# A Hymba decoder step: leaving the 16 meta tokens out of the stages that only feed y

## The chip, the cores and the metric

The kernel runs on one core of a Trainium2 chip. The metric is the device time of one execution in microseconds (us); lower is better. The engines are TensorE (PE; its weight loads are listed as PEld), VectorE (DVE), ScalarE (ACT), GpSimd (POOL) and SyncE (SP), which issues nearly all DMAs.

## The reference

One decoder layer with shared weights for a prompt of 1024 tokens, in front of which 16 learned meta tokens are put, and for 8 sample tokens with their own states. Together 1048 tokens of width 1024, float32:

```
h += 0.5 * SwiGLU_1(rmsnorm(h))              # 1024 -> 2816 -> 1024
u  = rmsnorm(h) @ w_in                       # q, f, i, g (4 heads of 128), z, x/B/C, dt
HGRN2, 4 heads: S_t = diag(f_t) S_{t-1} + k_t v_t^T, o_t = S_t^T q_t
                out = rmsnorm(o) * w * silu(g)
Mamba-2, 8 heads of 64: conv(4) + silu on x/B/C, scan over the tokens, y_t = h_t C_t + D x_t
                out = rmsnorm(y * silu(z)) * w
h += concat(hgrn, mamba) @ w_out
h += 0.5 * SwiGLU_2(rmsnorm(h))
y = rmsnorm(h)                               # the 16 meta tokens are dropped from y_prompt
```

Outputs are y for the prompt and the samples, and the states after the last token. The meta tokens reach the outputs only through the two recurrences and the convolution: through f, k = 1 − f, i, x, B, C and dt of their positions. Their q, g and z, their rows of the output projection, of the second FFN and of the last norm reach no output.

## The kernel before

All activations stand with the 128 features of a block on the partitions and tokens along the free axis, in the order meta, prompt, samples: T = 1048 columns. Tiles of the pool `big` are 1056 columns wide, 30 with the tag `u` and 8 with the tag `s`.

**Products.** A float32 product is made of three matmuls in float32r (`mm3`, lines 141 to 146): high part of the weights by high part of the tokens (line 144), high by low (145), low by high (146). The weights are split on ScalarE (cast, 138) and VectorE (subtraction, 139), so are the tokens. Each matmul loads 128x128 weights and streams the token columns of one chunk.

**The two FFNs** (`ffn`, line 743) use one level of Strassen's scheme in Winograd's form: seven products where a plain split would have eight. The tokens are cut into four quarters of Q = T/4 = 262 columns; quarters (0, 1) and (2, 3) make two lanes, and the scheme joins the quarters of a lane. `pair` (462) makes gate and up of 128 hidden features: 7 products, each of 4 blocks of 128 for either lane, 262 columns at a time. There are 22 pairs. The products are put together on VectorE by `post` (485), multiplied by the norm's factors (`times_r`, 480), and the hidden values are stored to DRAM by `Hidden` (558). `down` (620) reads them back for each of the 7 products of the down projection (`DORDER`), splits them (607, 611) and adds the results to the tiles of h (697). The order of the FFN's instructions on PE, DVE, ACT and SP is written out by hand as steps (`Steps`, 352): `S.before(i, fn)` puts work ahead of step i. `first2` (1854) and `after3` (1904) place the start and the end of the second FFN. After the last product `Final` (1584) and `LastFinal` (1617) transpose h by tiles of 128 tokens, make the last norm and store y; `token_rows` (867) says which rows of a tile go to which output. Tiles 4, 5 and 6 come last.

**The mixer** stands between the FFNs and is ordered by a scheduler, which interleaves projections and scans. `proj` (335) makes one unit of 128 output features in three chunks of columns, (0, 350), (350, 350), (700, 348), with 8 x 3 matmuls each. `ssm_project` (1002) makes x, B and C (8 units) and dt, `ssm_scan` (1142) the Mamba scan in nine chunks of tokens, `ssm_gate` (1288) the four units of z and their gate on y, `ssm_norm` (1306) the grouped norm. For each of the four heads `hgrn_project` (1328) makes q, f and i, `hgrn_scan` (1384) the recurrence over 1040 tokens, a second call of `hgrn_project` the gate g, and `hgrn_out` (1541) norm and gate. The projections that wait their turn fill TensorE between the steps of the scans. The parts of the eight samples are jobs on GpSimd (for HGRN lines 1528 to 1530, read by the matmuls of line 1533) that are slipped in. Two of the four gated heads and two of the tiles of y are spilled to DRAM (`spill`, 1789) and read back split (`split_spilled`, 1792). `out_proj` (1561) multiplies by w_out a quarter at a time and adds to h (1574), which was spilled after the first FFN and is loaded again (1825); `Norm` (187) makes the factors of the second FFN's norm.

Of the kernel before, what the change touches and what calls it, by code (L numbers as in the profile page):

```python
# [29 lines left out]
CHUNKS = [(0, 350), (350, 350), (700, 348)]  # L30
CW = 350
# [33 lines left out]
class Core:  # L65
    def __init__(self, ctx, tc):
# [10 lines left out]
        self.n = 0  # L77
        self.banks_ = ent(ExitStack())
        self.banks(1)

# [90 lines left out]
def rstd_wide(K, v, r, after):  # L171
# [4 lines left out]
    with K.tc.issue_after(ld.ins):  # L176
        parts = [(v[:, s : s + T // 2], r[:, s : s + T // 2]) for s in (0, T // 2)]
# [9 lines left out]
class Norm:  # L187
# [8 lines left out]
    def r(self, q):  # L196
        if self.spread:
            return self.spread.quarter(q)
        return self.rt[q // 2][:, (q % 2) * Q : (q % 2) * Q + Q]

    def add(self, k, q):
        K = self.K
        hs = self.h[k][:, q * Q : q * Q + Q]
        if q not in self.sq:
            self.sq[q] = K.t(Q)
            self.an = K.nc.scalar.activation(self.sq[q], hs, AF.Square)
        else:
            t = K.t(Q)
# [3 lines left out]
    def begin(self, q, table=True):  # L212
        K = self.K
        if not self.spread and q // 2 not in self.rt:
            self.rt[q // 2] = K.t(2 * Q)
        ps = K.psm()
        K.nc.tensor.matmul(ps[:, :Q], K.ones[D], self.sq[q], start=True, stop=True)
        self.newton[q] = K.rstd(self.r(q), ps[:, :Q], Q, self.an if table else None)
# [8 lines left out]
    def begin_half(self, half):  # L227
# [3 lines left out]
        ps = [K.psm()[:, :Q] for i in range(2)]  # L231
        r, l = K.t(2 * Q), K.t(2 * Q)
        for i in range(2):
            nc.tensor.matmul(ps[i], K.ones[D], self.sq[2 * half + i], start=True, stop=True)
            nc.scalar.activation(l[:, i * Q : i * Q + Q], ps[i], AF.Ln, bias=K.eps)
        nc.scalar.activation(r, l, AF.Exp, scale=-0.5, bias=K.lna)

        def newton():
            nc.vector.scalar_tensor_tensor(l, r, -1.0, r, ALU.mult, ALU.mult)
            for i in range(2):  # L240
                li = l[:, i * Q : i * Q + Q]
                nc.vector.scalar_tensor_tensor(li, ps[i], EPS, li, ALU.add, ALU.mult)
            out = self.spread.tile()[:, half * 2 * Q : half * 2 * Q + 2 * Q]
# [5 lines left out]
class Spread:  # L249
# [6 lines left out]
    def tile(self):  # L256
        if self.t is None:
            self.t = self.K.slot("u", T)
        return self.t

    def quarter(self, q):
        return self.tile()[:, q * Q : q * Q + Q]
# [10 lines left out]
def plain_x(K, norm, wcol, q):  # L273

    cs = slice(q * Q, q * Q + Q)
    xn = {}

    def job(k):
        if k < KT:
            xn[k] = K.t(Q)  # L280
# [16 lines left out]
class Blocks:  # L297
# [6 lines left out]
    def new(self, p):  # L304
        self.b[p] = self.K.slot("u", T)
        return self.b[p]

    def scaled(self, h, wcol, ps):

        for p in ps:  # L310
# [3 lines left out]
            for k in range(4):  # L314
                self.K.nc.scalar.activation(t[:, k * Q : k * Q + Q], h[k0 + k][:, q * Q : q * Q + Q], AF.Identity, scale=wcol[:, k0 + k : k0 + k + 1])
# [7 lines left out]
    def cast(self, p):  # L323
        hi = self.K.slot("u", T, F32R)
# [3 lines left out]
    def low(self, p):  # L328
        hi = self.op[p][0]
        lo = self.K.slot("u", T, F32R)  # L330
# [4 lines left out]
def proj(K, wh, wl, evac, chunks=(0, 1, 2)):  # L335

    for c in chunks:
        c0, w = CHUNKS[c]
# [6 lines left out]
def proj_first(K, units):  # L345

    for c in range(3):
# [78 lines left out]
class Unit:  # L426
# [6 lines left out]
    def bank(self, p, cs, mis):  # L433

        b = {2: 1, 3: 5, 4: 7}.get(p, p)
        if (b, cs) not in self.ps:
            K = self.K
            if len(cs) == 2:
                self.ps[b, cs] = K.psum2()[:, :, :Q]
            else:  # L440
                self.ps[b, cs] = (K.psm() if mis and b == 7 else K.psum())[:, None, :Q]
# [20 lines left out]
def pair(K, S, wg, wu, f, ops, spread, hid, late_r, first=None):  # L462
# [12 lines left out]
    def temp(n, cs):  # L475
        if n not in tm:
            tm[n] = halves(K.t(2 * Q))
# [41 lines left out]
    def product_(n, cs):  # L519
        if "h" not in tm:  # L520
            tm["h"] = True
            hid.append(K.slot("s", T))
        nc.vector.tensor_mul(halves(hid[0][:, n * 2 * Q : n * 2 * Q + 2 * Q])[:, cs], temp(f"g{n}", cs), temp(f"u{n}", cs))
# [34 lines left out]
class Hidden:  # L558


    def __init__(self, K):
        self.K = K
        self.d = {p: K.dram.tile([P, 2, FP, Q], F32, name=K.uid("hd")) for p in ORDER}

    def jobs(self, S, i, hid, e0, e1):
# [4 lines left out]
        def block(n):  # L570

            return hid[n // 2][0][:, n % 2 * 2 * Q : n % 2 * 2 * Q + 2 * Q]
# [4 lines left out]
        def sub(p, x, y):  # L577
            s = {5: 0, 6: 0, 7: 1, 4: 1}[p]
            if s not in t:
                t[s] = K.slot("s", T)  # L580
            o = (p in (6, 4)) * 2 * Q
            b[p] = t[s][:, o : o + 2 * Q]
# [12 lines left out]
    def load(self, S, p, at):  # L595
# [4 lines left out]
        def load(g, c):  # L600
            i, n = GROUPS[g]
            op[c][g] = K.slot("u", n * Q, F32R), K.slot("u", n * Q, F32R)
# [17 lines left out]
def down(K, S, wdv, hidden, src, h, after):  # L620
# [6 lines left out]
    def tiles(j):  # L627
        for _ in range(2):
            h.append(K.slot("s", T))
            hs.append(h[-1].rearrange("p (c n t) -> p c n t", c=2, n=2))  # L630

    def residual(o, at):
        box = []

        def load():
            box.append(K.slot("u", T))
# [66 lines left out]
    for a, p in enumerate(DORDER):  # L703
# [6 lines left out]
        if a < 6:  # L710
            for j in range(KT // 2):
                box = []
                for g in range(3):
                    pieces(p, j, g, b + 6 * j + 2 * g, None)
                    for c in range(2):

                        def mm(p=p, j=j, g=g, c=c, op=op, box=box):
                            if not box:
                                box.append(K.psum2()[:, :, :Q])
# [3 lines left out]
        else:  # L723
# [6 lines left out]
            for c in range(2):  # L730
                for j in range(KT // 2):
                    box = []
                    for g in range(3):

                        def mm(p=p, j=j, g=g, c=c, op=op, box=box):
                            if not box:
                                box.append(K.psum()[:, :Q])
# [1223 lines left out]
```

## Time and profile before

| | us |
|---|---|
| median of 3 runs (2028.59 to 2029.81) | 2029.59 |
| the profiled execution | 2029.82 |
| its span, first to last instruction | 2028.1 |

The page of the profile gives the busy time of each engine, the chain of work that ended last, and the costliest groups of instructions with line, tiles and shapes (partitions x elements). The views of the trace that are used below: busy time of the engines in stretches of the span, given in us from its start, with the number of instructions in brackets; groups of instructions by form; waits of an engine by what ended them (total, times, longest); the instructions of one engine in order of time. TensorE's granted clock is a share of full speed. Records of matmuls overlap each other: the next starts before the last has ended.

### The profile page before, as it was taken

The page shows a single profiled execution, that of the slowest core. Times are in us where ns is not written, and L with a number is a line of the kernel's source. Part 1 is how long each engine was busy: PE and PEld are TensorE (multiplying, and loading weights), DVE is VectorE, ACT ScalarE, POOL GpSimd, SP SyncE. Part 2 cuts the span into 40 slices and gives each one's busy share as a digit, 9 for nine tenths or more (in the row PEclk, how much of TensorE's full clock was granted, in tenths as well). Part 3 has the DMA queues.
Part 4 walks back from the last instruction along what each step waited for, and adds up shares of the span by engine and source line. Part 5 has one row for each costly group of instructions (what it writes and reads, how often), then busy time and mean ns, then how long its engine had stood idle before and what let it go on. Part 6 is the DMA issues. An engine that isn't in the chain of part 4 may idle for free.

```text
span 2028.1 us, 40739 instructions
## 1 busy us (share of the span) xinstructions
PE 1958.5 (97%) x16647; PEld 1912.4 (94%) x16647; DVE 1468.5 (72%) x2437; ACT 822.3 (41%) x1528; POOL 153.2 (8%) x197
## 2 busy tenths in 40 slices
PE   6999999999999999979999999999999999999997
PEld 6999999999999999968989889999999999999997
DVE  7777777777688686598454556887777777768973
ACT  6522222224534553564534444752222222354352
POOL 3000000000002210231010111200000000000000
PEclk8999999999999999999999999999999999999999
DMA  6233342325976621263120335224232333587851
GB/s 213 74 98 98 94 113 83 108 80 169 316 237 195 201 85 34 93 188 93 50 76 12 107 100 187 84 80 121 85 111 80 102 105 92 160 238 241 269 174 69
DMA packets 323890, 259.32 MB, mean 128 GB/s; under 512 B 17584, under 2 KB 299440, under 8 KB 323696
## 3 DMA queue, kind: packets, MB, share of 16 engines
q1 hardware_dynamic: 323464, 256.68, 41.8%
q8 instruction: 131, 2.15, 0.4%
q14 instruction: 55, 0.45, 0.1%
q0 software_dynamic: 224, 0.04, 0.0%
q10 hardware_dynamic: 16, 0.00, 0.0%
HBM read 191.26 MB, written 65.47 MB: 127 GB/s over the span
## 4 chain that ended last, share of the span: by engine, by line
PE 78%; DVE 11%; DMA 4%; issue 2%; ACT 2%; SPq 1%; POOL 0%; DVEq 0%; ACTq 0%; POOLq 0%
PE acc L144 24%; PE acc L146 24%; PE acc L145 24%; DMA r<-in_w_ffn_up_dram 1%; DVE u L332 1%; DVE u L611 1%; DMA s<-in_x_prompt_dram 1%; DVE ws L673 1%; DVE ws L402 1%; DMA r<-in_w_in_dram 1%; DVE s L697 1%; DVE s L640 1%; DMA r<-in_w_ffn_down_dram 1%; DVE t L482 1%; DMA s<-cumd 0%
## 5 line engine op out<-in xcount | busy, mean ns | idle before, releaser
L144 PE MATMUL acc<-u,ws 128*128 128x262 f32 (+2 forms) x4504 | 1319.2, 293 | 16.5 <-ACT ws L138 4.8
L145 PE MATMUL acc<-u,ws 128*128 128x262 f32 (+2 forms) x4504 | 1312.2, 291 | 5.6 <-DVE u L332 3.8
L146 PE MATMUL acc<-u,ws 128*128 128x262 f32 (+2 forms) x4504 | 1313.4, 292 | 2.9 <-DVE ws L402 2.9
L144 PEld LDWEIGHTS acc<-u,ws 128*128 128x128 f32 x4504 | 854.8, 190 | 21.2 <-issue 7.1
L145 PEld LDWEIGHTS acc<-u,ws 128*128 128x128 f32 x4504 | 857.9, 190 | 9.5 <-DVE u L332 5.1
L146 PEld LDWEIGHTS acc<-u,ws 128*128 128x128 f32 x4504 | 853.2, 189 | 5.6 <-DVE ws L402 4.3
L402 DVE TENSOR_TENSOR ws<-r,ws 128x512 fp32r<-128x512 f32 x308 | 212.8, 692 | 79.0 <-ACT ws L398 79.0
L398 ACT CAST ws<-r 128x512 fp32r<-128x512 f32 x308 | 173.8, 614 | 4.8 <-DVE r L394 4.6
L517 ACT ACTIVATE t<-t 128x524 f32<-128x524 f32 x47 | 30.1, 643 | 304.6 <-DVE t L482 304.6
L394 DVE TENSOR_TENSOR r<-r,r 128x512 f32<-128x512 f32 x176 | 121.1, 690 | 11.6 <-DMA r<-in_w_ffn_up_dram 10.0
L210 POOL TENSOR_TENSOR t<-t,t 128x262 f32<-128x262 f32 x56 | 55.3, 998 | 775.0 <-ACT t L209 775.0
L494 ACT ACTIVATE t<-t 128x524 f32<-128x524 f32 x41 | 26.3, 642 | 203.1 <-DVE t L482 203.1
L611 DVE TENSOR_TENSOR u<-u,u 128x1048 fp32r<-128x1048 f32 (+1 forms) x84 | 97.8, 1166 | 10.4 <-ACT u L607 10.4
L139 DVE TENSOR_TENSOR ws<-r,ws 128x512 fp32r<-128x512 f32 x88 | 65.8, 756 | 44.1 <-ACT ws L138 43.8
L482 DVE TENSOR_TENSOR t<-t,u 128x524 f32<-128x524 f32 x135 | 90.9, 701 | 2.8
L607 ACT CAST u<-u 128x1048 fp32r<-128x1048 f32 (+1 forms) x84 | 83.3, 994 | 1.4 <-DMA u<-hd 1.4
L668 ACT CAST ws<-u 128x512 fp32r<-128x512 f32 (+1 forms) x72 | 42.1, 585 | 101.0 <-DVE u L663 95.7
L697 DVE SCALAR_TENSOR_TENSOR s<-acc,s 128x524 f32<-128x524 f32 (+1 forms) x88 | 55.8, 649 | 37.4 <-PE acc L146 36.7
L673 DVE TENSOR_TENSOR ws<-r,ws 128x512 fp32r<-128x512 f32 (+1 forms) x84 | 57.3, 693 | 29.8 <-ACT ws L668 29.8
L138 ACT CAST ws<-r 128x512 fp32r<-128x512 f32 x88 | 53.9, 616 | 54.2 <-PE acc L146 28.5
L668 ACT CAST ws<-r 128x512 fp32r<-128x512 f32 (+1 forms) x84 | 47.4, 581 | 66.2 <-DVE r L663 37.2
L487 ACT COPY t<-acc 128x524 f32<-128x524 f32 (+1 forms) x46 | 26.6, 577 | 107.2 <-PE acc L146 107.2
(388 smaller groups left out, 1893.4 us busy)
## 6 DMA issues: line engine op xcount, KB each, us to landing
hd<-s SPq DMA_DIRECT2D x170, 262.0 KB
u<-hd SPq DMA_DIRECT2D x64, 524.0 KB
r<-in_w_ffn_down_dram SPq DMA_DIRECT2D x128, 256.0 KB
r<-in_w_ffn_gate_dram SPq DMA_DIRECT2D x88, 256.0 KB
r<-in_w_ffn_up_dram SPq DMA_DIRECT2D x88, 256.0 KB
r<-in_w_in_dram SPq DMA_DIRECT2D x56, 256.0 KB
r<-in_w_ffn_down_dram SPq DMA_DIRECT2D x64, 192.0 KB
u<-hd SPq DMA_DIRECT2D x28, 393.0 KB
```

Of the source, the lines that this page charges most:

```text
L144: mm(ps, whi, xhi, start=first, stop=False, skip_group_check=more)
L145: mm(ps, whi, xlo, start=False, stop=False, skip_group_check=more)
L146: mm(ps, wlo, xhi, start=False, stop=last, skip_group_check=more)
L394: self.K.nc.vector.tensor_tensor(self.raw[p], self.raw[x], self.raw[y], op)
L398: self.K.nc.scalar.copy(self.w[p][:, : self.n * P], self.raw[p])
L402: self.K.nc.vector.tensor_sub(t[:, 512 : 512 + w], self.raw[p], t[:, :w].bitcast(F32))
L482: nc.vector.tensor_mul(t, t if src is None else src, spread.lanes(i, cs))
L607: K.nc.scalar.copy(hi, lo.bitcast(F32))
L611: K.nc.vector.tensor_sub(lo, lo.bitcast(F32), hi.bitcast(F32))
L668: nc.scalar.copy(w[p, j, g][:, : n * P], src)
L673: nc.vector.tensor_sub(t[:, 512 : 512 + n * P], box[0], t[:, : n * P].bitcast(F32))
L697: nc.vector.scalar_tensor_tensor(t, b, 0.5, t, ALU.mult, ALU.add)
```

## The change

The meta tokens are left out where their values reach no output. TO = T − 16 = 1032 columns.

- Units of q, g and z use chunks of 344 columns that begin at column 16; f, i, x, B, C and dt keep the three chunks of before.
- The first 16 columns of q are set to zero on GpSimd, and the scan goes over the same 1040 tokens. The gated heads, the norms of the mixer and the spills have 1032 columns; y is used from column 16 on.
- Ahead of the output projection `K.tokens(TO)` sets the number of tokens to 1032 and the quarter to 258. Everything that follows takes the quarter from K: output projection, norm, all blocks of the second FFN, its hidden values in DRAM, residual and last norm. h is loaded from column 16 on.
- The tiles of the last norm then begin with the prompt: tile 0 stores 128 rows, tile 8 the eight samples.

Cut to its core (the many places that only write `K.Q` and `K.T` for `Q` and `T` are left out):

```diff
+TO = T - NM
+CHUNKS_O = [(NM, 344), (NM + 344, 344), (NM + 688, 344)]
...
+    def tokens(self, n):
+        self.T, self.Q = n, n // 4
...
-def proj(K, wh, wl, evac, chunks=(0, 1, 2)):
-    for c in chunks:
-        c0, w = CHUNKS[c]
+def proj(K, wh, wl, evac, chunks=CHUNKS):
+    for c0, w in chunks:
...
 def product(K, ps, w, op, n, first, last, more=False):
     for k in range(n):
-        ks = slice(k * Q, k * Q + Q)
+        ks = slice(k * K.Q, k * K.Q + K.Q)
...
 def token_rows(i, prompt, sample):
-    t0 = P * i - NM
-    if i == 0:
-        return [(NM, P - NM, prompt[0 : P - NM, :])]
     if i < 8:
-        return [(0, P, prompt[t0 : t0 + P, :])]
-    return [(0, NM, prompt[t0:SEQ, :]), (NM, NS, sample)]
+        return [(0, P, prompt[P * i : P * i + P, :])]
+    return [(0, NS, sample)]
...
 def ssm_gate(K, a, g):
-    for c in range(3):
+    for c in CHUNKS_O:
...
 def ssm_norm(K, g, tag):
-    ya, yb = K.y[2 * g], K.y[2 * g + 1]
-    v, r = K.slot(tag, w=T), K.slot(tag, w=T)
+    ya, yb = (K.y[2 * g + i][:, NM:] for i in range(2))
+    v, r = K.slot(tag, w=TO), K.slot(tag, w=TO)
...
 def hgrn_project(K, a, hd, which, jobs=3):
-        nc.scalar.activation(out["g"][:, c0 : c0 + w], ps, AF.Silu)
+        nc.scalar.activation(out["g"][:, c0 - NM : c0 - NM + w], ps, AF.Silu)
...
-                (ev_q if x == "q" else ev_f)(0, T, out[x])
+                c0 = NM if x == "q" else 0
+                (ev_q if x == "q" else ev_f)(c0, T - c0, out[x][:, c0:])
...
-        out[x] = K.slot("u", w=T)
+        out[x] = K.slot("u", w=TO if x == "g" else T)
+        if x == "q":
+            nc.gpsimd.memset(out[x][:, :NM], 0.0)
...
-        proj(K, *ahead[i], evs[x])
+        proj(K, *ahead[i], evs[x], CHUNKS_O if x in "qg" else CHUNKS)
...
 def hgrn_scan(K, a, o, hd, u):
-        pieces.append((po, 512 * half, 512))
+        c0 = NM if half == 0 else 0
+        pieces.append((po[:, c0:], 512 * half + c0 - NM, 512 - c0))
...
 def body(ctx, tc, a, o):
-                spill(2 + i, K.y[i])
+                spill(2 + i, K.y[i][:, NM:])
...
-    kept += K.y[2:]
+    kept += [y[:, NM:] for y in K.y[2:]]
+    K.tokens(TO)
     h = []
     for k in range(KT):
-        t = K.slot("s", T)
-        nc.sync.dma_start(t, hsp[k * P : (k + 1) * P, :])
+        t = K.slot("s", TO)
+        nc.sync.dma_start(t, hsp[k * P : (k + 1) * P, NM:])
```

More of the change, by code (lines that the diff above doesn't have):

```diff
@@ L240, in newton @@
             for i in range(2):
[L241 removed]
+                li = l[:, i * self.K.Q : i * self.K.Q + self.K.Q]
                 nc.vector.scalar_tensor_tensor(li, ps[i], EPS, li, ALU.add, ALU.mult)
[L243 removed]
+            out = self.spread.tile()[:, half * 2 * self.K.Q : half * 2 * self.K.Q + 2 * self.K.Q]
             nc.vector.scalar_tensor_tensor(out, l, 3.0 * 2.0 ** (-2.0 / 3.0), r, ALU.add, ALU.mult)
@@ L345, in proj_first @@
 def proj_first(K, units):
-    for c in range(3):
+    for c in CHUNKS:
         for wh, wl, evac in units:
@@ L562, in __init__ @@
         self.K = K
-        self.d = {p: K.dram.tile([P, 2, FP, Q], F32, name=K.uid("hd")) for p in ORDER}
+        self.d = {p: K.dram.tile([P, 2, FP, self.K.Q], F32, name=K.uid("hd")) for p in ORDER}
     def jobs(self, S, i, hid, e0, e1):
@@ L1319, in ssm_norm @@
     rstd_wide(K, v, r, an)
-    for i in range(2):
-        y = K.y[2 * g + i]
+    for i, y in enumerate((ya, yb)):
         nc.vector.scalar_tensor_tensor(y, y, K.pc["ssm_norm"][:, 2 * g + i : 2 * g + i + 1], r, ALU.mult, ALU.mult)
@@ L1786, in body @@
     constants_mix(K, a)
-    md = K.dram.tile([D // 2, T], F32, name="mspill")
+    md = K.dram.tile([D // 2, TO], F32, name="mspill")
     def spill(i, t):
@@ L1834, in body @@
     nf2 = Norm(K, h, spread2)
-    hd2 = [K.dram.tile([P, T], F32, name=K.uid("hd")) for k in range(KT)]
+    hd2 = [K.dram.tile([P, TO], F32, name=K.uid("hd")) for k in range(KT)]
     def keep2(half):
         for k in range(KT):
-            cs = slice(half * 2 * Q, half * 2 * Q + 2 * Q)
+            cs = slice(half * 2 * K.Q, half * 2 * K.Q + 2 * K.Q)
             nc.sync.dma_start(hd2[k][:, cs], h[k][:, cs])
```

87 lines of the change are left out of this document (44 added, 43 removed).

## The prediction

> **What bounds the kernel now.** I read the page first, for the busy shares and for the chain that ended last, then the busy time of each engine in stretches that follow the stages.
>
> ```profile
> span 2028.1 us, 40739 instructions
> ## 1 busy us (share of the span) xinstructions
> PE 1958.5 (97%) x16647; PEld 1912.4 (94%) x16647; DVE 1468.5 (72%) x2437; ACT 822.3 (41%) x1528; POOL 153.2 (8%) x197
> ```
>
> ```profile
> ## 4 chain that ended last, share of the span: by engine, by line
> PE 78%; DVE 11%; DMA 4%; issue 2%; ACT 2%; SPq 1%; POOL 0%; DVEq 0%; ACTq 0%; POOLq 0%
> ```
>
> TensorE is busy for 97% of the span and the chain that ended last is TensorE for 78%. The weight loads (PEld) are busy for almost as long. That leaves two readings of the bound: the columns that stream through the array, or the weight loads. They have to be told apart, because the change takes away columns and no weight load.
>
> ```profile
> core 0: us, PE busy (x) PEld busy (x) DVE busy (x) ACT busy (x) POOL busy (x), PEclk, DMA share, GB/s
> 493.00:830.00 337.00, 334.38 (x2529) 326.97 (x2528) 253.60 (x430) 155.76 (x280) 33.48 (x40) 1.00 0.54 164
> 830.00:1240.00 410.00, 383.08 (x4081) 354.29 (x4080) 248.86 (x486) 199.35 (x384) 75.09 (x77) 0.97 0.34 101
> 1240.00:1300.00 60.00, 59.23 (x482) 58.69 (x481) 44.13 (x80) 35.73 (x66) 10.59 (x14) 1.00 0.42 133
> 1300.00:1342.00 42.00, 39.50 (x317) 38.75 (x317) 38.76 (x54) 29.58 (x58) 13.82 (x14) 1.00 0.23 77
> 1342.00:1778.00 436.00, 434.14 (x3549) 433.35 (x3548) 332.12 (x515) 122.89 (x219) 0.00 (x0) 1.00 0.35 104
> 1778.00:2004.00 226.00, 224.37 (x1844) 223.78 (x1843) 166.51 (x265) 97.53 (x165) 0.00 (x0) 1.00 0.68 208
> 2004.00:2028.10 24.10, 11.73 (x91) 10.47 (x89) 11.18 (x34) 7.05 (x29) 0.00 (x0) 0.84 0.28 112
> ```
>
> The stretches are: end of the first FFN and the shared projections (493 to 830), the state-space scan with the four HGRN heads (830 to 1240), output projection (1240 to 1300), start, products and down projection of the second FFN (1300 to 2004), last tail. From 1342 to 2004 TensorE is busy for 99.3 to 99.6% at full granted clock, with VectorE at 74 to 76%: there the time is TensorE's alone. In the scan stretch TensorE is idle for 410.0 − 383.1 = 27 us; there a saving of matmul time may be lost in a wait.
>
> Busy time doesn't give the price of one matmul, as the records overlap. The count in a clean stretch does:
>
> ```profile
> 1081.00:1111.00 30.00, 30.00 (x189) 30.00 (x188) 13.08 (x18) 11.88 (x23) 2.76 (x2) 1.00 0.05 18
> ...
> 1400.00:1500.00 100.00, 100.00 (x821) 100.00 (x820) 76.33 (x119) 25.61 (x47) 0.00 (x0) 1.00 0.32 95
> ```
>
> ```profile
> L144 PE MATMUL acc<-u,ws 128*128 128x262 f32 x274 | 78.2, 285 | 0.0
> ```
>
> ```profile
> L144 PE MATMUL acc<-u,ws 128*128 128x350 f32 x46 | 14.9, 323 | 0.0
> ...
> L144 PE MATMUL acc<-u,ws 128*128 128x348 f32 x17 | 5.5, 322 | 0.0
> ```
>
> The row of 1400 to 1500 holds only matmuls of 262 columns, that of 1081 to 1111 only those of 350 (46 a line) and 348 (17 a line), 349.5 on average. Each count takes in about two that began before the stretch (a record lasts about 0.3 us by the rows, a little over two spacings), so the spacing is 100/819 = 122.1 ns at 262 columns and 30/187 = 160.4 ns at 349.5. Both stretches show the clock at 1.00. The difference, 38.3 ns for 87.5 columns, is **0.438 ns a column**, and 122.1 − 262 × 0.438 = 7.3 ns do not depend on the columns.
>
> **The change part by part.** Three groups of matmuls lose columns; how many there are comes from the rows by form (lines 145 and 146 have the same counts as line 144):
>
> ```profile
> L144 PE MATMUL acc<-u,ws 128*128 128x262 f32 x3832 | 1096.3, 286 | 11.4 <-DVE t L496 3.9 <-ACT u L326 2.4 <-DVE t L498 1.8
> ...
> L144 PE MATMUL acc<-u,ws 128*128 128x350 f32 x448 | 148.4, 333 | 5.2 <-ACT ws L138 4.8 <-ACT u L282 0.4
> ...
> L144 PE MATMUL acc<-u,ws 128*128 128x348 f32 x224 | 74.5, 333 | 0.0
> ...
> L144 PE MATMUL acc<-u,u 128*128 128x262 f32 x88 | 25.2, 286 | 0.0
> ...
> L144 PE MATMUL mis<-u,ws 128*128 128x262 f32 x32 | 9.4, 295 | 0.1
> ```
>
> - Second FFN. 22 pairs × 7 products × 4 blocks × 2 lanes × 3 = 3696, and the down products 7 × 4 × 11 × 2 × 3 = 1848, together 5544 matmuls. They go from 262 to 258 columns: 5544 × 4 × 0.438 = **9.7 us**. Both FFNs and the output projection make 3 × (3832 + 88 + 32) = 11,856 in the rows, which is 2 × 5544 + 768, so the count agrees.
> - Output projection: the 768, 262 to 258: 768 × 4 × 0.438 = **1.3 us**.
> - Queries, gates, z: 12 of 28 units (3 × (448 + 224) = 2016 = 28 × 72 matmuls), each 16 columns less over its three chunks, in 24 matmuls: 12 × 24 × 16 × 0.438 = **2.0 us**.
>
> Sum: 29,856 column passes less, 13.1 us. The form of 258 columns isn't in the trace, so its price is bounded: at most 122.1/262 = 0.466 ns a column (spacing in proportion to the width), 13.9 us; at the low end nothing, if weight loads set the spacing, or less than nothing, if the new block addresses cost something (both below). I take 0.438, since it is the difference of two rows of this same loop with the same weight loads.
>
> The Trainium skill, TensorE: Matmul & The Clock Gate, section Back-to-back issue gap, gives for a stream of weight load and matmul about 81 ns at 128 columns and about 131 ns at 512, and for the isolated gap N/2.4 + 2.5 ns. By the isolated form the sum would be 29,856/2.4 = 12.4 us, by the stream 29,856 × 50/384 = 3.9 us (estimates from that page). The trace speaks against the stream figure here: 160.4 ns at 349.5 columns lies above its value for 512.
>
> What is off the path. Every VectorE and ScalarE operation on tokens in these stages has 1.5% fewer elements; VectorE is at 38.8 of 42.0 us in 1300 to 1342, at most 0.6 us there, and elsewhere TensorE's time covers it. I count nothing. The last tail (2004 to 2028) is the norm of token tiles 4 to 6; tile limits stay multiples of 128, and quarters of 258 end at 258, 516 and 774, so each tile waits for the same quarters as before. I leave it as it is. The first tile stores 128 rows and not 112, the last one 8 in one store and not 24 in two: not in the last chain, nothing.
>
> What is added: one memset of 16 columns on GpSimd for each of the four heads. The nearest row is the 128x16 memset at 0.11 us:
>
> ```profile
> 743.25 0.11 POOL L1121 MEMSET s<- 128x16 f32 x1
> ...
> 1125.50 1.49 POOL L1529 TENSOR_TENSOR r<-r,qs 128x512 f32<-128x512 f32 x1
> ```
>
> ```profile
> L1790 SPq DMA_DIRECT2D mspill<-u x4: 319/339/339, 987.0 to 1089.3; - x4
> ```
>
> In the built program three of the four wait for nothing that isn't long over (matmuls and a copy of the shared projections); the fourth waits for the spill of y to DRAM and stands between the state products of a head (line 1528 ahead of it, line 1529 behind). Queued behind it are lines 1529 and 1530, which the sample matmuls of TensorE (line 1533) wait for. The spill is issued at 987 at the earliest (four stores, the last of them at 1089.3, are of this line), the products run at 1125.5, so the wait is over by then: 4 × 0.11 us on an engine that is 8% busy, nothing. Without that cover it would cost whatever the store is late beyond 1125. The 16 zero columns of q then go through the scan as before, so the scan keeps its work.
>
> Moved are also the loads of h, which now start 64 bytes into each row:
>
> ```profile
> L1825 SPq DMA_DIRECT2D s<-hspill x8: 320/423/521, 1215.2 to 1225.8; - x8
> ...
> who waited for it (us, times):
> ```
>
> Nobody waited for them (the line after the colon is empty), and SP's queue keeps its order in the built program, with one store fewer at the end: no DMA is moved past another. In the scan stretch the scheduler shifts single matmuls between the steps of the scan (13 before a step become 14, 12 become 13, in about a dozen places), and a few neighbours on VectorE and ScalarE change places; no other engine has more instructions than before, GpSimd has four.
>
> Now the part of the 2.0 us of the projections that may be lost:
>
> ```profile
> PE mis L1454 <- DVE u L1469: 8.4, 7, 1.9
> PE mis L1185 <- DVE s L1181: 4.9, 4, 1.5
> PE acc L144 <- ACT ws L138: 4.8, 1, 4.8
> PE mis L1445 <- DVE u L1469: 3.0, 3, 1.7
> ```
>
> These are TensorE's longest waits in 830 to 1240. The matmuls of the next head are fillers between scan steps that VectorE paces; a shorter filler only brings TensorE to the wait earlier. In the built program about a quarter of a head's projection matmuls stand as fillers (runs of 5 to 15 between steps), the rest in blocks of some 200. A quarter of 2.0 is 0.5 us; half of it lost is 0.2. **Sum: 13.1 − 0.2 = 12.9 us.** The profiled execution took 2029.8 us (span 2028.1 and 1.7 around it); 2029.8 − 12.9 = **2016.9 us**. The median of the runs, 2029.59, lies 0.2 us under the profiled one, which is within what single runs differ.
>
> **The rivals.**
> - *The mix gives nothing* (chance 0.17). The projections sit beside VectorE's scan; all of their 2.0 us goes into longer waits, and the shifted matmuls cost up to 1.5 us more (one wait such as line 1454's, longest 1.9). For it: 27 us of idle time there, and a scheduler that decides the order. Against it: most projection matmuls stand in full blocks. Time: 2029.8 − 11.1 = 2018.7, up to 2020.2.
> - *The spacing doesn't follow the columns* (0.06): at 262 columns the weight loads set it, so that the change doesn't save what it says. For it: PEld is busy 100.00 of 100 us in the row of 1400, with 820 loads of 128 columns that stay. Against: PEld is also 30.00 of 30 at 349.5 columns and the spacing is 38 ns longer, so a full PEld row doesn't prove that it paces. Only the projections, whose form is wide, would gain: 2029.8 − 2.0 = 2027.8, within 0.2%. By the skill's stream figure of above it would be 2029.8 − 3.9 = 2025.9, in the same class.
> - *The new block addresses slow the reads* (0.04), on the other side. Blocks within a tile begin every 1032 bytes and no longer every 1048. If the 7.3 ns that do not depend on the columns are a cost of reading the moving operand, and it grows with the new starts, 6312 matmuls (5544 + 768) pay it. It decides from 13.1 us/6312 = 2.1 ns, that is a spacing over 122.4 ns at 258 columns. With half as much again, 3.7 ns: 6312 × 3.7 − 13.1 = +10.3, 2040.1 us. Against: 262 columns already start at bytes that differ from block to block, and both wide chunks start at others, without a sign of it in the two spacings.
> - *More than the sum* (0.05): spacing in proportion and the 0.6 us at the start of the second FFN: 2029.8 − 13.9 − 0.6 = 2015.3; with a shift in the scan that happens to help, 2014.8.
>
> **How the numbers follow.** The forecast itself has 0.68, from 2015.9 (13.9 us) to about 2018. The range takes in the first and the last rival, 2014.8 to 2020.2; left out are the second and third, 0.10, and I leave it at that width as nothing in the profile makes the bounds wider. Within 0.2% is about what a measurement of this kernel can't tell from no change, 4.1 us. Faster by more: 0.68 + 0.17 + 0.05 = 0.90. Within: 0.06. Slower by more: 0.04.
>
> **What would show it.** In the changed kernel a clean stretch of 100 us in the products of the second FFN should count about 833 matmuls of 258 columns (spacing 122.1 − 1.75 = 120.3 ns, and two at the edge) instead of 821; a block of gate or query projection at 344 columns should be spaced by about 158.0 ns. All up to the scan (830) should stand where it stood; the output projection should start about 1.8 us earlier, the second FFN about 3.1 us earlier, the end 12.9. A spacing still at 122 shows the second rival, one over 122.4 the third; a start of the output projection that isn't earlier shows the first. Sample matmuls of line 1533 that wait for GpSimd would show the memset wrong.

## The result and the profile after

| | changed | before | ratio (95% interval) |
|---|---|---|---|
| first comparison, medians of 6 runs each | 2011.1 us (2008.48 to 2015.86) | 2030.86 us | 0.9905 (0.9891 to 0.992) |
| profiled execution | 2015.86 us, span 2014.1 | 2029.82 us, span 2028.1 | |

The forecast was 2016.9 us, 12.9 less, with a range from 2014.8 to 2020.2. The change is faster, by more than that: 19.8 us between the medians of this comparison, which lies outside of the range, and 14.0 us between the two spans. Three later comparisons of the same kernel (below) gave ratios of 0.9926 to 0.9927, 13.6 to 15.9 us between the medians. So there are two questions: why the traces differ by 14 us and not by 13, and why the first comparison gave nearly 20.

The page of the changed kernel, first its busy times, then the chain that ended last:

```profile
span 2014.1 us, 40751 instructions
## 1 busy us (share of the span) xinstructions
PE 1944.5 (97%) x16647; PEld 1897.0 (94%) x16647; DVE 1458.3 (72%) x2437; ACT 819.4 (41%) x1528; POOL 158.0 (8%) x201
...
## 4 chain that ended last, share of the span: by engine, by line
PE 80%; DVE 11%; DMA 3%; issue 3%; ACT 2%; SPq 0%; POOL 0%; DVEq 0%; ACTq 0%; POOLq 0%
```

The picture is that of before, TensorE 97% busy and 80% of the chain. Busy time per stretch (columns as before: TensorE, weight loads, VectorE, ScalarE, GpSimd, granted clock, DMA share, GB/s), cut 14 us earlier at the end:

```profile
830.00:1240.00 410.00, 383.39 (x4100) 354.37 (x4099) 246.97 (x490) 198.91 (x384) 77.75 (x80) 0.97 0.34 101
1240.00:1300.00 60.00, 59.21 (x488) 58.68 (x487) 44.24 (x80) 37.75 (x69) 10.46 (x14) 1.00 0.40 127
1300.00:1342.00 42.00, 39.44 (x318) 38.49 (x317) 39.44 (x56) 27.80 (x56) 13.69 (x14) 1.00 0.25 83
1342.00:1778.00 436.00, 432.89 (x3600) 431.70 (x3599) 334.81 (x521) 125.15 (x224) 0.00 (x0) 1.00 0.35 103
1778.00:1990.00 212.00, 211.03 (x1762) 210.47 (x1761) 156.38 (x252) 92.14 (x158) 0.00 (x0) 1.00 0.71 219
1990.00:2014.10 24.10, 12.16 (x95) 10.92 (x94) 11.16 (x34) 7.49 (x31) 0.00 (x0) 0.86 0.29 116
```

No stage has a new wait: 432.9 of 436 us busy in the products (434.1 before), 383.4 of 410 in the mixer (383.1). The output projection starts 1.9 us earlier than before and the second FFN 3.1 us earlier, where 1.8 and 3.1 were forecast; for the mixer so close a hit is luck, as its time changes by some 6 us from trace to trace of one kernel (below). More matmuls fit into the same stretch, 3600 where there were 3549. In stretches of 100 us of the second FFN:

```profile
1350.00:1450.00 100.00, 100.00 (x837) 100.00 (x836) 78.70 (x124) 27.42 (x50) 0.00 (x0) 1.00 0.31 92
1450.00:1550.00 100.00, 98.90 (x824) 98.55 (x823) 75.56 (x119) 26.90 (x50) 0.00 (x0) 1.00 0.34 98
1600.00:1700.00 100.00, 100.00 (x836) 100.00 (x835) 75.98 (x119) 27.42 (x50) 0.00 (x0) 1.00 0.35 103
```

837 for 821 means, without the two at the edge, 100/835 = 119.8 ns a matmul; the forecast was 833 and 120.3. The stretch from 1450 has 1.1 us without a matmul and counts 824, so a single stretch doesn't do for tenths. I therefore took the mean interval between starts of successive matmuls of one width over the whole stage, leaving out intervals more than a quarter over the median (0.6% of them in the second FFN). That gives 121.99 and 122.03 ns at 262 columns in two traces of before, 119.91 to 119.92 at 258 in four of the changed kernel, and in its mixer 160.5 at 350, 159.5 at 348 and 157.3 at 344 (forecast 158.0).

The forms moved as the prediction counted them (lines 152 to 154 are the old 144 to 146): 2044 + 1788 is the 3832 of before, and 288 = 12 × 24 are the narrow projections.

```profile
L152 PE MATMUL acc<-u,ws 128*128 128x258 f32 x2044 | 578.8, 283 | 6.2 <-DVE t L504 2.9 <-ACT t L495 1.4 <-DVE t L506 1.0
...
L152 PE MATMUL acc<-u,ws 128*128 128x262 f32 x1788 | 512.2, 286 | 4.9 <-ACT u L335 2.4 <-DVE t L506 0.9 <-DVE s L705 0.9
...
L152 PE MATMUL acc<-u,ws 128*128 128x344 f32 x288 | 97.4, 338 | 4.5 <-ACT ws L146 4.5
```

The four memsets cost 0.11 us each, and the fourth, whose cover the prediction argued, waited for nothing. The first did wait 7.73 us, for a matmul that the prediction took to be long over, on an engine with nothing else to do:

```profile
773.39 0.11 POOL L1379 MEMSET u<- 128x16 f32 x1 [7.73 <-PE mis L1087]
...
953.51 0.11 POOL L1379 MEMSET u<- 128x16 f32 x1
...
1065.32 0.11 POOL L1379 MEMSET u<- 128x16 f32 x1
...
1125.26 0.11 POOL L1379 MEMSET u<- 128x16 f32 x1
```

One wait of TensorE is put down to a memset, the first line here; before, the same matmul waited as long for the addition that runs just ahead of the memset (second line):

```profile
PE mis L1322 <- POOL u L1379: 1.5, 1, 1.5
```

```profile
PE mis L1317 <- POOL s L1313: 1.5, 1, 1.5
```

### The profile page after: what moved, and what is told of

It is laid out like the page before. It is cut to its first block, busy times and chain, and to the rows that moved or that the text cites. A ratio compares the mean times of both kernels' runs of the same rounds, so it can differ in the third digit from the quotient of the medians.

```text
span 2014.1 us, 40751 instructions
## 1 busy us (share of the span) xinstructions
PE 1944.5 (97%) x16647; PEld 1897.0 (94%) x16647; DVE 1458.3 (72%) x2437; ACT 819.4 (41%) x1528; POOL 158.0 (8%) x201
## 4 chain that ended last, share of the span: by engine, by line
PE 80%; DVE 11%; DMA 3%; issue 3%; ACT 2%; SPq 0%; POOL 0%; DVEq 0%; ACTq 0%; POOLq 0%
PE acc L152 25%; PE acc L154 25%; PE acc L153 24%; DMA r<-in_w_ffn_up_dram 1%; DVE u L341 1%; DMA s<-in_x_prompt_dram 1%; DVE u L619 1%; DVE ws L681 1%; DVE s L705 1%; DMA r<-in_w_in_dram 1%; DVE ws L410 1%; DVE s L648 1%; DMA r<-in_w_ffn_down_dram 1%; PE mis L1190 0%; PE mis L1503 0%
## 5 line engine op out<-in xcount | busy, mean ns | idle before, releaser
L152 PE MATMUL acc<-u,ws 128*128 128x258 f32 (+4 forms) x4504 | 1311.9, 291 | 16.0 <-ACT ws L146 4.5
L154 PE MATMUL acc<-u,ws 128*128 128x258 f32 (+4 forms) x4504 | 1308.3, 291 | 3.2 <-DVE ws L410 3.2
L153 PE MATMUL acc<-u,ws 128*128 128x258 f32 (+4 forms) x4504 | 1305.8, 290 | 5.2 <-DVE u L341 4.2
L525 ACT ACTIVATE t<-t 128x524 f32<-128x524 f32 (+1 forms) x47 | 29.9, 640 | 301.3 <-DVE t L490 301.2
L219 POOL TENSOR_TENSOR t<-t,t 128x262 f32<-128x262 f32 (+1 forms) x56 | 57.7, 1040 | 771.7 <-ACT t L218 771.7
L502 ACT ACTIVATE t<-t 128x516 f32<-128x516 f32 (+1 forms) x41 | 26.2, 639 | 200.9 <-DVE t L490 200.9
L619 DVE TENSOR_TENSOR u<-u,u 128x1048 fp32r<-128x1048 f32 (+3 forms) x84 | 97.0, 1157 | 10.4 <-ACT u L615 10.4
L490 DVE TENSOR_TENSOR t<-t,u 128x524 f32<-128x524 f32 (+1 forms) x135 | 90.3, 697 | 2.9
L615 ACT CAST u<-u 128x1048 fp32r<-128x1048 f32 (+3 forms) x84 | 82.8, 988 | 1.4 <-DMA u<-hd 1.4
L705 DVE SCALAR_TENSOR_TENSOR s<-acc,s 128x524 f32<-128x524 f32 (+3 forms) x88 | 54.6, 643 | 37.1 <-PE acc L154 36.8
L495 ACT COPY t<-acc 128x524 f32<-128x524 f32 (+3 forms) x46 | 26.4, 575 | 105.8 <-PE acc L154 105.8
```

Source lines behind the costliest of these rows:

```text
L152: mm(ps, whi, xhi, start=first, stop=False, skip_group_check=more)
L153: mm(ps, whi, xlo, start=False, stop=False, skip_group_check=more)
L154: mm(ps, wlo, xhi, start=False, stop=last, skip_group_check=more)
L490: nc.vector.tensor_mul(t, t if src is None else src, spread.lanes(i, cs))
L615: K.nc.scalar.copy(hi, lo.bitcast(F32))
L619: K.nc.vector.tensor_sub(lo, lo.bitcast(F32), hi.bitcast(F32))
```

## The experiments

**Theories.** (1) Columns and clock: the gain is the columns' (13 to 14 us); what goes beyond it is chance, from stretches of 3.4 us at half TensorE clock whose number changes from run to run. (2) Rival: the narrow mixer gives some 8 us in every run. (3) Rival: the second FFN gains more than its columns.

**The kernel before and the changed one again** (no edit), and each part of the change alone.

> The kernel before, unchanged, as a control. Theory of columns and clock (the columns give 13 us, what was measured beyond it comes from stretches of 3.4 us at half TensorE clock in the scan stage, whose number changes from run to run): times between 2028 and 2033 us, the granted clock between 0.988 and 0.990, six such stretches between 830 and 1240 us of the span. Rival (the narrow mixer gives some 8 us whatever the clock does): the same times, and no relation of time and clock.

Measured: 2031.23 us (11 runs, 2027.95 to 2034.92), ratio 0.9998 (0.9988 to 1.0009). These eleven runs of one kernel spread over 7 us, those of before beside it over 9; the three runs known at first spread over 1.2 us.

> The changed kernel, unchanged, once more, for a second trace and the clock of each run. Theory of columns and clock: times spread over 2008 to 2016 us, and a run is shorter by about 1.7 us for each half-clock stretch of 3.4 us that it lacks (0.001 of mean clock less than 2 us apart); matmul for matmul the second FFN gains the same 10 us as in the first trace. Rival (mixer gives 8 us): in this trace the mixer is 6 to 8 us shorter than before at the same number of half-clock stretches.

Measured: 2016.79 us (2012.99 to 2021.77), ratio 0.9927 (0.9912 to 0.9942). The runs lie higher than the 2008 to 2016 us that were expected.

Tail only: chunks, norms and heads of the mixer as before, slices from column 16 on where they are spilled and kept.

```diff
-    for c in CHUNKS_O:
+    for c in CHUNKS:
...
-        proj(K, *ahead[i], evs[x], CHUNKS_O if x in "qg" else CHUNKS)
+        proj(K, *ahead[i], evs[x], CHUNKS)
...
-            spill(hd, u["g"])
+            spill(hd, u["g"][:, NM:])
```

> Only the part of the change from the output projection on: queries, gates, z and the mixer's norms are computed on all 1048 tokens as before, then 1032 tokens in quarters of 258. Theory of columns and clock: 11.0 us by columns (9.7 + 1.3), so 2019 to 2020 us against 2030.9, and about 5 us less only in runs that lack half-clock stretches. Rival (the mixer gives 8 us): 2019 to 2020 us in every run, as the mixer is unchanged. Third theory (the second FFN itself is worth more than its columns): below 2016 us.

Measured: 2017.18 us, ratio 0.993 (0.9913 to 0.9947), between the 2019 to 2020 us of theory (1) and the 2016 of theory (3).

Mixer only: the other half, with no `K.tokens(TO)` and q and g zeroed in 16 columns.

```diff
-        if x == "q":
+        if x in "qg":
             nc.gpsimd.memset(out[x][:, :NM], 0.0)
...
-    K.tokens(TO)
```

> Only the part in the mixer: q, g, z and the mixer's norms on 1032 tokens (the first 16 columns of q and g are zeroed), everything from the output projection on for 1048 tokens as before. Theory of columns and clock: 2.0 us by columns, 2029 us, and lower by 1.7 us for each half-clock stretch that is missing in the scan. Rival (the mixer gives 8 us): 2022 to 2024 us in every run. Third theory (gain in the second FFN): 2029 us whatever the clock.

Measured: 2029.25 us (12 runs), ratio 0.9986 (0.9975 to 0.9997), some 3 us. Rival (2) falls: neither does the mixer alone give 8 us, nor does the tail alone lack them.

Time by stage in the traces, cut at the same matmul in each (us; in brackets the us at half clock in the stage):

| trace | up to the mixer | mixer | output projection | second FFN | after the last product |
|---|---|---|---|---|---|
| before | 724.4 | 488.0 (23.9) | 108.4 | 696.1 | 11.2 |
| before again | 724.8 | 484.8 (17.1) | 108.6 | 696.8 | 11.2 |
| tail only | 723.7 | 487.5 (23.9) | 107.2 | 685.3 | 10.8 |
| mixer only | 723.7 | 487.9 (20.5) | 108.7 | 698.8 | 11.2 |
| changed | 724.5 | 486.0 (23.9) | 107.2 | 685.8 | 10.7 |
| changed again | 724.8 | 483.1 (17.1) | 107.2 | 685.4 | 10.8 |
| changed, third | 725.5 | 489.7 (30.7) | 107.2 | 686.1 | 10.7 |
| changed, fourth | 723.3 | 486.2 (20.5) | 107.2 | 686.8 | 10.8 |

Second FFN: 697.2 us on the mean of the three traces with the old tail, 685.9 on that of the five with the new one, 11.3 us, and no trace is further than 1.6 from its mean. Output projection 1.4. The mixer varies by 6 us with the kernel unchanged, and its time goes with the time at half clock. A straight-line fit over these and five more traces (13 in all) gives 0.34 us more for each us at half clock and 1.2 ± 0.7 us less for the narrow projections at equal clock. That the two go together doesn't show which is the cause: half clock draws out the matmuls (in the changed kernel those of 262 columns follow each other at 0.22 us at half clock, 16 us after the start, and at 0.12 us at 24 us), but a wait of TensorE may as well bring on half clock. Such stretches look like this in the third trace, and make the mixer of that trace slower than that of the second:

```profile
866.00:869.40 3.40, 3.40 (x20) 2.86 (x19) 3.40 (x10) 2.61 (x5) 3.40 (x5) 0.56 0.51 158
904.00:910.80 6.80, 3.38 (x15) 2.68 (x16) 4.81 (x14) 4.09 (x10) 0.00 (x0) 0.50 1.05 299
959.00:965.80 6.80, 6.71 (x112) 6.27 (x113) 3.36 (x7) 2.53 (x6) 0.00 (x0) 0.53 1.00 268
```

```profile
724.50:1210.00 485.50, 457.17 (x4460) 424.07 (x4463) 299.63 (x620) 225.76 (x444) 80.92 (x92) 0.97 0.26 77
```

```profile
724.50:1210.00 485.50, 457.98 (x4538) 424.80 (x4539) 306.54 (x627) 230.44 (x455) 81.94 (x92) 0.98 0.28 81
```

The first fence holds three pieces of the third trace: the granted clock is 0.50 to 0.56, and in the one from 904 TensorE is busy for only 3.4 of 6.8 us. The other two hold the whole mixer of the third trace, at 0.97 with 4460 matmuls in 485.5 us, and of the second, at 0.98 with 4538. Over all runs of all kernels tried, with one constant for each kernel and occasion, the time falls by 1.5 ± 0.1 us for each 0.001 of mean clock, with 2.1 us left over. The Trainium skill, TensorE: Matmul & The Clock Gate, part 1 on the clock gate, says that the gate works in free-running windows of 3413 ns and halves the clock after an idle one. The traces agree on the window, as their half-clock pieces last 3.41 us or a multiple of it. That the window ahead has to be idle they don't show: in the third trace TensorE has work in 1.2 to 1.7 us of the 3.4 ahead of the pieces at 866, 904 and 1136, and in all of it ahead of the one at 1156:

```profile
862.95:866.36 3.41, 1.19 (x12) 0.74 (x10) 2.37 (x3) 3.41 (x11) 2.71 (x3) 1.00 1.05 315
900.50:903.90 3.40, 1.47 (x8) 0.99 (x8) 3.40 (x10) 2.90 (x8) 0.00 (x0) 1.00 0.78 214
1132.60:1136.00 3.40, 1.74 (x71) 1.46 (x71) 2.88 (x6) 0.00 (x0) 0.24 (x1) 1.00 0.62 160
1153.10:1156.50 3.40, 3.40 (x23) 2.73 (x23) 0.99 (x2) 0.83 (x3) 0.10 (x1) 1.00 0.73 200
```

**Does the gain depend on columns alone?** Theory (3) remained, for some 2.1 ns a matmul at four columns fewer is more than the 1.75 forecast. First the kernel before, with its operand addresses, and with the width alone cut in the second FFN (the last four columns of each quarter are left incomplete):

```diff
+        hi, lo = op[0][:, ks], op[1][:, ks]
+        if K.cut and not (first and k == 0):
+            ps, hi, lo = ps[:, : Q - 4], hi[:, : Q - 4], lo[:, : Q - 4]
+        K.mm3(ps, wh, wl, hi, lo, first and k == 0, last and k == n - 1, more)
```

> The kernel before, with the operands of the second FFN where they were (blocks every 262 columns), but the matmuls stream only the first 258 columns of a block, except the first three of each accumulation. The last four columns of each quarter are so left incomplete. 4848 of 5544 matmuls are narrower. If the width alone sets the price: spacing of 119.9 ns at 258 columns as in the changed kernel, 4848 x 2.09 = 10.1 us less than before. If the block addresses of the change (every 1032 bytes and not 1048) gave the part above 0.438 ns a column: spacing of 120.2 to 120.4 ns, 8.5 us less.

Measured: spacing 120.35 ns at 258 columns and 121.5 at the 262 that were left, 2025.7 us, ratio 0.998 (0.9963 to 0.9996). The spacing is the one that the theory of addresses had named. The second FFN took 691.2 us, 6.0 less than before and not 8.0 (4848 × 1.65), as some 2 us more fell into the longer intervals. Then the changed kernel with the old distance of blocks, width 258 (`K.S` is 262, and the operand tiles are padded to it):

```diff
-        ks = slice(k * K.Q, k * K.Q + K.Q)
+        ks = slice(k * K.S, k * K.S + K.Q)
```

> The changed kernel, but the blocks of the second FFN's token operands begin every 262 columns (1048 bytes) as before the change, with four columns of padding; width 258. If the addresses give the part of the gain above 0.42 ns a column: spacing up from 119.9 to 120.35 ns as in the kernel with the same addresses, 5544 x 0.43 = 2.4 us slower than the changed kernel. If the width alone does: 119.9 ns, no difference in TensorE's stretches.

Measured: 120.15 ns, 686.4 us in the second FFN, 2017.1 us, ratio 0.9927 (0.9904 to 0.9951). The spacing lies half-way between the two expectations; in time no difference from the changed kernel beside it (2017.11) could be told.

> The changed kernel with blocks every 264 columns (1056 bytes, so that starts are multiples of 32 bytes), width 258. If starts on rounder addresses are read faster, as the first block of a tile (118.9 ns against 119.7 to 120.7 for the other three) and the quarters of 256 suggest: spacing of 118.5 to 119.2 ns, 5544 x 0.7 to 1.4 = 4 to 8 us less than the changed kernel. If only the width counts: 119.9 ns and no gain, perhaps 1 us lost on VectorE and ScalarE in the longer access patterns.

Measured (`K.S = 264`): 120.25 ns and no gain, 687.4 us in the second FFN, 2017.02 us, ratio 0.9929 (0.9913 to 0.9944). Rounder starts aren't what helps; that theory fell. Even the first block of a tile, which begins at the tile's start in both, took 118.9 ns in the changed kernel and 120.5 here. Count of matmuls in 100 us, in this order: same addresses, distance 262, distance 264, quarters of 256.

```profile
1350.00:1450.00 100.00, 100.00 (x832) 100.00 (x831) 77.45 (x121) 29.42 (x54) 0.00 (x0) 1.00 0.31 92
```

```profile
1350.00:1450.00 100.00, 100.00 (x835) 100.00 (x835) 78.58 (x124) 27.42 (x50) 0.00 (x0) 1.00 0.31 91
```

```profile
1350.00:1450.00 100.00, 100.00 (x833) 100.00 (x832) 78.44 (x124) 27.41 (x50) 0.00 (x0) 1.00 0.31 91
```

```profile
1350.00:1450.00 100.00, 100.00 (x850) 100.00 (x849) 78.12 (x123) 28.26 (x53) 0.00 (x0) 1.00 0.33 101
```

So at one distance of 262, cutting 262 to 258 columns gives 1.7 to 1.9 ns (0.42 to 0.47 ns a column, around the 0.438 of the prediction), and something else in the change gives another 0.2 to 0.4. What that is stays open. It isn't the roundness of the starts, and the distance of the blocks isn't needed for it: the two kernels with a distance of 262 differ by 0.2 themselves, and in the kernel before the first FFN takes 121.7 ns where the second takes 122.0, at equal widths and distances. The clearest case is this first FFN, whose widths and distances are the same in all kernels. Its spacing is 121.70 to 121.74 ns in fifteen traces and 121.97 in the kernel with extra matmuls (below). In that one, as built, all of its results and nearly all of its weights lie where they lie in the others, but 2924 of its 5544 matmuls read their tokens from other buffers, and extra matmuls run ahead of it. In 100 us, the changed kernel and that one:

```profile
140.00:240.00 100.00, 100.00 (x825) 100.00 (x824) 75.36 (x118) 27.54 (x50) 0.00 (x0) 1.00 0.34 96
```

```profile
140.00:240.00 100.00, 100.00 (x822) 100.00 (x822) 76.03 (x118) 27.04 (x50) 0.00 (x0) 1.00 0.33 97
```

Two narrower tails (`TT = 1024` and `TT = 1008` columns from column 16 on, so quarters of 256 and 252; rows of y for the samples, and in the second also for the last 16 prompt tokens, are left out), and other chunks in the mixer:

> The changed kernel with 1024 tokens in quarters of 256 from the output projection on: the last eight columns, the samples, are left out of y (the samples' rows of y are filled from the last prompt tokens). Price of 0.52 ns a column going on: spacing of 118.9 ns, 6312 x 1.04 = 6.6 us less than the changed kernel. Price of 0.438: 119.0 ns, 5.5 us. Stepped price with a step at 256 columns: 116 to 117 ns, 15 to 20 us less.

Measured: 117.99 ns, 2002.14 us, ratio 0.9864 (0.9839 to 0.9888). The two columns from 258 to 256 gave 1.9 ns, neither of the named values but between them; the second FFN took 675.8 us.

> As with quarters of 256, but 252: 1008 tokens, the last 16 of the prompt and the samples are left out of y (their rows are filled from other tokens). One look at the price under 256 columns. If the price goes on: spacing of 116 to 117.5 ns, 6312 x 2.5 = 13 to 24 us less than the changed kernel. If matmuls under 256 columns run in a slower mode: spacing well above 118 ns, up to several times as long.

Measured: 116.50 ns, so no slower mode; but 2026.87 us, in its one run. The second FFN took 670.9 us, as the columns have it, and the output projection 130.5 us instead of 105.7. The scheduler of the mixer had set another order (5 and 4 filler matmuls in the last head's scan where it set 12 and 12, and the norm's matmuls nearer to their sums), and TensorE then waited at a reduced clock. The waits of TensorE from 1205 to 1320 and a stretch of it:

```profile
PE acc L153 <- DVE s L1583: 9.7, 5, 3.4
PE mis L227 <- POOL t L220: 4.7, 2, 3.3
```

```profile
1280.00:1320.00 40.00, 31.67 (x236) 30.92 (x237) 25.70 (x42) 23.88 (x41) 1.43 (x2) 0.91 0.22 67
```

> The changed kernel with other chunks in the mixer's projections: 384, 368, 296 where it had 350, 350, 348, and 448, 320, 264 where it had 344 three times. One look, for the spacing of matmuls at six more widths. Theory of one line (7.3 ns and 0.438 ns a column): 122.9 ns at 264, 136.9 at 296, 147.5 at 320, 168.5 at 368, 175.5 at 384, 203.5 at 448. Theory of a stepped price (0.52 to 0.55 ns a column between near widths as 262 and 258, 350 and 344, and falls somewhere between 262 and 344): spacings that lie off that line by 1 to 3 ns, in the same way for widths with the same remainder by some power of two.

```diff
-CHUNKS = [(0, 350), (350, 350), (700, 348)]
+CHUNKS = [(0, 384), (384, 368), (752, 296)]
-CHUNKS_O = [(NM, 344), (NM + 344, 344), (NM + 688, 344)]
+CHUNKS_O = [(NM, 448), (NM + 448, 320), (NM + 768, 264)]
```

Measured: 121.5 ns at 264, 134.6 at 296, 147.0 at 320, 167.5 at 368, 173.6 at 384, 204.6 at 448; 2011.95 us in its one run. The points lie 1.1 ns over to 2.3 ns under the line of the prediction. No order by remainders is to be seen; 264 columns at one place took less than 262 at another. The slope over 88 columns was good for the width, but what four columns are worth is no larger than this scatter. The mixer of this trace took 479.5 us, some 5 us less than the fit gives for its 16.6 us at half clock, and the output projection 2 us more; with a single run, whether such chunks are worth taking isn't shown.

**Is the clock worth keeping up?** Six extra matmuls ahead of the first transposes, of each chunk of the Mamba scan and of the last head's levels:

```diff
+    def warm(self, ps, n):
+        for _ in range(n):
+            self.nc.tensor.matmul(ps[:, :P], self.ident, self.ones[1], start=True, stop=True)
...
+        K.warm(py, 6)
```

> The changed kernel with small extra matmuls (identity by ones, 128 columns, overwritten by what follows) ahead of the first transposes, of the scan's products and of the last head's levels, six each, so that TensorE is busy where it waited. If the differences from run to run come from the granted clock and that from TensorE's idle stretches: mean clock from 0.989 to 0.993 or more, fewer half-clock stretches, smaller spread, and 3 to 6 us less than the changed kernel, less whatever extra matmuls fall where TensorE wasn't idle (160 x 0.11 = 17 us at most). If the clock only goes along with other causes: the clock rises and the time doesn't fall, 2015 to 2030 us.

Measured: 2039.89 us, ratio 1.0045 (1.0028 to 1.0063), a miss. The first 24 us have full clock, but the first product begins 8 us later (at 22.1 us, in the changed kernel at 13.7), behind the extra matmuls; mixer and output projection take 622 us for 593. In this trace the clock of the mixer is lower, not higher:

```profile
0.00:24.00 24.00, 21.33 (x164) 21.19 (x165) 9.62 (x22) 10.31 (x20) 13.58 (x52) 1.00 0.84 275
...
830.00:1240.00 410.00, 380.74 (x4078) 351.80 (x4077) 232.41 (x460) 181.90 (x361) 76.42 (x80) 0.96 0.31 90
```

This trace is of the run with the lowest mean clock of the eleven (0.987). Their mean is 0.9903, no higher than in the first comparison of the changed kernel and a little over the later ones (0.9885 to 0.9900). And the price of the extra matmuls was set too low: each of the 156 stands in the trace as two matmuls of 0.11 us or more, 312 in all where 160 were counted, and the 192 of these in the mixer and at its end take over 20 us. So this run doesn't settle whether the clock causes the spread.

**Chance or not?** Two more comparisons of the changed kernel and one of the tail.

> The changed kernel once more, on another occasion, because the first two comparisons gave ratios of 0.9905 and 0.9927. The traces so far sum to 14.2 us between the kernels (11.0 in the second FFN, 1.4 in the output projection, 1.8 in the mixer). If what lay beyond 14.2 us at first was chance of the granted clock: 14 to 16 us less than before, ratio 0.992 to 0.993. If the change has a gain that the traces miss: 18 to 20 us, ratio 0.9905.

Measured: 2017.11 us, before 2030.67, ratio 0.9926 (0.9909 to 0.9943).

> The changed kernel again. If the first comparison (19.3 us, ratio 0.9905) was chance of the granted clock around a true 14 to 15 us: ratio 0.992 to 0.9935, and the same time as the others at the same clock (about 2015 us at 0.990). If the change has a gain in unprofiled runs that the traces miss: 0.990 to 0.991.

Measured: 2015.39 us, before 2031.25, ratio 0.9926 (0.9905 to 0.9946).

> The part from the output projection on, again, on the same chip as the changed kernel. By the traces it gives 12.4 us of the 14.2: ratio 0.9935 to 0.994, 1 to 3 us slower than the changed kernel beside it. If the mixer's part were worth more in unprofiled runs: 4 us or more slower than the changed kernel.

Measured: 2016.25 us, ratio 0.9936 (0.9917 to 0.9955), 0.9 us over the changed kernel beside it; the mixer isn't worth more outside of the traces.

The 24 runs of the changed kernel have a mean of 2015.3 us with a spread (standard deviation) of 4.0, 84 runs of the kernel before 2031.0 with 3.1: 15.7 us, with some 0.9 of uncertainty if the occasions are taken as one. Without the first comparison it is 14.7. The traces sum to 11.3 + 1.4 + 1.2 + 0.4 = 14.3. The first comparison had the higher mean clock (0.9903; the later ones 0.9885 to 0.9900), which at 1.5 us for 0.001 goes with up to 3 us of its lead; at equal clock it still lies 2.8 to 4.4 us under the later ones, with an uncertainty of 0.9 on each. That rest wasn't seen again, and its cause stays open. So theory (1) holds for most of the 14 to 16 us that the later comparisons show, and theory (3) for the 1.6 us by which the second FFN gained more than forecast. For what the first comparison had beyond that, chance is likely and goes in part with the clock, but neither is shown for all of it.

## Why the prediction was wrong

- **What bounds the kernel: right.** TensorE's columns; the weight loads don't pace, as the spacing fell with the columns in every variant though each matmul kept its load. The rival of a spacing that doesn't follow the columns falls. The Trainium skill, TensorE: Matmul & The Clock Gate, section Back-to-back issue gap, would by its stream figure have given 3.9 us, which falls with it; its isolated form gives 1.67 ns for four columns (both estimates from that page), beside 1.7 to 1.9 measured at one distance of blocks.
- **Second FFN, 9.7 us: mis-sized.** Measured 11.3 in the traces. The step that failed here is the price of a column, taken from two widths of the same loop as 0.438 ns and bounded at 0.466: in the changed kernel four columns gave 2.09 ns, 0.52 a column. 1.7 to 1.9 of it is width. The rest, 0.2 to 0.4, came with where the operands lie or with something that goes along with it; the prediction had that only as a risk (its third rival, with the sign the other way), and had no row to bound it.
- **Output projection, 1.3 us: right** (1.4). **Mixer, 1.8 us after the part lost: about right**, 1.2 ± 0.7 in the traces at equal clock, 3 us by its own runs with an interval from 0.6 to 5.
- **Nothing for the last tail:** 0.4 us was there. **Memsets, stores, loads of h: right**, nothing.
- **The range: the step that failed most.** It adds up costs of the kernel alone, from the one profiled execution, and puts the scatter of runs at nothing, although the same text calls 4.1 us what a measurement of this kernel can't tell from no change. The three runs known lay within 1.2 us. In their place the runs showed that six executions of the changed kernel on one occasion spread by 7 to 12 us, and 22 of the kernel before by 15. The clock row of 0.97 in the mixer and the idle time of 27 us there were quoted, but read as room for a lost gain, not as a source of spread. The sum of the traces, 2029.8 − 14.3 = 2015.5 us, and the later medians, 2015.4 to 2017.1 us, lie in the range; the first, 2011.1, lies 3.7 us under it. That is scatter only in part: at equal clock the first comparison stays 2.8 to 4.4 us under the later ones, and the cause of this stays open.

## What to carry to other kernels

Where TensorE is busy for over 99% at full clock and columns reach no output, count the matmuls and take the spacing from counts in clean stretches: that gave 12.9 us of 14.3, stage by stage. Leave out a token range in whole stages, and check how the scheduler orders what lies between: in one run here a few columns fewer came with another order and 25 us more. Before a range is written, run the old kernel often enough to see its own spread, and ask which stage it sits in: here the mixer, which runs below full clock in places, differs by 6.6 us between traces of one kernel, and the second FFN by 1.5.

## What the runs showed of the hardware

- The float32r matmuls of this loop are spaced by 116.5, 118.0, 119.9 and 122.0 ns at 252, 256, 258 and 262 columns: no slower mode shows at 252.
- At equal width the mean spacing differs by 0.2 to 0.4 ns from program to program (119.9, 120.15, 120.25, 120.35 ns at 258 columns; 121.7 and 122.0 at 262), and repeats to some 0.04 ns from trace to trace of one program. Equal widths and distances of blocks don't make it equal (121.72 and 121.97 ns in the first FFN of two programs).
- Records of weight loads fill 100% of the clean stretches at 256, 258, 262 and 349.5 columns, while the spacing goes from 118.0 to 160.4 ns: a full row of weight loads doesn't show that they set the pace.
